# Log-softmax over 50,000 columns: tiles of every second row in place of neighbouring rows, and 40 empty instructions taken out

## The chip, the core and the metric

The kernel runs on one core of one Trainium2 chip. The metric is the device time of the whole program in microseconds (us). The core has five engines with queues of their own (TensorE, VectorE, ScalarE, GpSimd, SyncE) and 16 DMA engines that move data between the chip's memory (HBM) and the on-chip memory (SBUF, 128 partitions).

## The reference

For each of 16 x 512 = 8192 rows of 50,000 float32 numbers, the logarithm of the softmax is computed: the row less its maximum, less the logarithm of the sum of the exponentials.

```python
batch, seq, vocab = 16, 512, 50000

def reference(x):
    max_x = np.max(x, axis=-1, keepdims=True)
    shifted = x - max_x
    log_sum_exp = np.log(np.sum(np.exp(shifted), axis=-1, keepdims=True))
    return (shifted - log_sum_exp).astype(np.float32)
```

The input is 1638.4 MB and the output as much. Each number is read once and written once. The rows are independent, so the order in which they are worked on is free.

## The kernel before

A tile is 32 rows. Each row is cut into G = 4 pieces of 12,500 numbers, so a tile fills 128 partitions with 12,500 numbers (50,000 B) each. There are 256 tiles and four buffers; tile t lives in buffer t modulo 4. SyncE issues the loads, VectorE takes the maxima, ScalarE takes the exponentials with their sums, TensorE adds the sums of the four pieces of a row, VectorE subtracts in place, and ScalarE issues the store.

```python
P = 128
G = 4
R = P // G            # 32 rows in a tile
C = 3125              # a quarter of a partition's 12500 columns
NBUF = 4
NS = 4
GATE = 2
PAUSE = 40
GS = G * NS           # 16 pieces of a row in a part of tile 0
RS = P // GS          # 8 rows in a part of tile 0

def take(engine, sem, n=16, pause=PAUSE):
    engine.wait_ge(sem, n)
    for _ in range(pause):
        engine.nop()
    engine.wait_ge(sem, n).then_inc(sem, -n)
```

`take` is how an engine waits for a transfer: a DMA raises a semaphore by 16 when it is done, and the engine that waits takes the 16 off again.

The views of input and output, whole tiles first and then the parts of tile 0, and the address of tile number 4q + first + i in a loop:

```python
    xt = xf.rearrange("(t r) (g w) -> t (r g) w", r=R, g=G)
    ot = of.rearrange("(t r) (g w) -> t (r g) w", r=R, g=G)
    xs = xf.rearrange("(t s r) (g w) -> t s (r g) w", s=NS, r=RS, g=GS)
    os = of.rearrange("(t s r) (g w) -> t s (r g) w", s=NS, r=RS, g=GS)

    def run(a, first, n):
        part = a[first : first + NBUF * n].rearrange("(q i) p w -> q i p w", i=NBUF)
        return lambda q, i: part[bass.ds(q, 1), i].rearrange("o p w -> (o p) w")
```

The loads. Tile 0 comes in four parts of 8 rows, each with a semaphore of its own, so that work can begin early. A later load into a buffer waits until the buffer's store is done.

```python
        for s in range(NS):
            sync.dma_start(out=bufs[0][:, cols(s)], in_=xs[0, s]).then_inc(landed_part[s], 16)
        for t in range(1, NBUF):
            load(t, xt[t])
        take(sync, stored[0], 16 * NS)
        load(0, xt[NBUF])
        src = run(xt, NBUF + 1, rounds - 1)
        with sync.Fori(0, rounds - 1) as q:
            for i in range(NBUF):
                j = (i + 1) % NBUF
                take(sync, stored[j])
                load(j, src(q, i))
        # ... the last loads and waits
```

VectorE on a tile (ScalarE's exponentials run beside it; TensorE's sums and ScalarE's logarithm come ahead of the subtraction):

```python
        def whole(j, by_pieces=False):
            take(vector, landed[j])
            for c in range(NS):
                vector.tensor_reduce(out=negms[j][:, c : c + 1], in_=bufs[j][:, cols(c)],
                                     op=ALU.max, axis=AX, negate=True)  # ... signals
            # ... the maximum over a row's four pieces, the rescaled sums
            subtract(j, *([bufs[j][:, cols(c)] for c in range(NS)] if by_pieces else [bufs[j]]))
```

ScalarE issues the store of one tile in the middle of its work on the next (`GATE`). Tile 0 is stored in four parts, like its load; the last tile is stored in four column pieces:

```python
        def store(j, dst, buf):
            subtracted.next(scalar.dma_start(out=dst, in_=buf)).then_inc(stored[j], 16)

        def whole(j, dst=None):
            for c in range(NS):
                if c == GATE and dst is not None:
                    store((j - 1) % NBUF, dst, bufs[(j - 1) % NBUF])
                # ... the exponential of a quarter, with its sum
            # ... scale, logarithm

        def in_parts(j, t):
            for s in range(NS):
                # ... the exponential of a part, with its sum
                if s:
                    store(j, os[t, s - 1], bufs[j][:, cols(s - 1)])
                log(NBUF + s)
            store(j, os[t, NS - 1], bufs[j][:, cols(NS - 1)])
        # ...
        for c in range(NS):
            store(NBUF - 1, ot[ntiles - 1][:, cols(c)], bufs[NBUF - 1][:, cols(c)])
```

Of the kernel before, what the change touches and what calls it, by code (L numbers as in the profile page):

```python
# [16 lines left out]
G = 4  # L17
R = P // G
C = 3125
NBUF = 4  # L20

NS = 4

GATE = 2

PAUSE = 40
GS = G * NS
RS = P // GS

# [16 lines left out]
        self.seen = 0  # L46


def take(engine, sem, n=16, pause=PAUSE):

    engine.wait_ge(sem, n)
    for _ in range(pause):
        engine.nop()
    engine.wait_ge(sem, n).then_inc(sem, -n)  # L54


def cols(c):
    return slice(c * C, (c + 1) * C)
# [3 lines left out]
def kernel(  # L62
# [6 lines left out]
    xf = x.flatten_outer_dims()  # L69
    of = out.flatten_outer_dims()  # L70
# [3 lines left out]
    ntiles = N // R  # L74


    rounds = (ntiles - NBUF) // NBUF
    assert ntiles % NBUF == 0 and rounds >= 2
    tail = range(1 + rounds * NBUF, ntiles)

    xt = xf.rearrange("(t r) (g w) -> t (r g) w", r=R, g=G)
    ot = of.rearrange("(t r) (g w) -> t (r g) w", r=R, g=G)
    xs = xf.rearrange("(t s r) (g w) -> t s (r g) w", s=NS, r=RS, g=GS)
    os = of.rearrange("(t s r) (g w) -> t s (r g) w", s=NS, r=RS, g=GS)

    def run(a, first, n):

        part = a[first : first + NBUF * n].rearrange("(q i) p w -> q i p w", i=NBUF)
        return lambda q, i: part[bass.ds(q, 1), i].rearrange("o p w -> (o p) w")

    data = ctx.enter_context(tc.tile_pool(name="data", bufs=1))
    stats = ctx.enter_context(tc.tile_pool(name="stats", bufs=1))
# [10 lines left out]
    bufs = [data.tile([P, W], FP32, name=f"buf{j}") for j in range(NBUF)]  # L103
# [41 lines left out]
    @block.gpsimd  # L145
    def _(gpsimd):
        k = 0
        for g in (GS, G):
            view = ones[g].rearrange("p (r g) -> p r g", g=g)
            r = P // g  # L150
            gpsimd.memset(ones[g], 1.0).then_inc(ready)
            gpsimd.affine_select(  # L152
                out=view, in_=view, pattern=[[-g, r], [0, g]], base=0,
                channel_multiplier=1, compare_op=ALU.is_ge, fill=0.0,
            ).wait_op(ready, k + 1, "sem-ge").then_inc(ready)
            gpsimd.affine_select(  # L156
                out=view, in_=view, pattern=[[g, r], [0, g]], base=g - 1,
                channel_multiplier=-1, compare_op=ALU.is_ge, fill=0.0,
            ).wait_op(ready, k + 2, "sem-ge").then_inc(ready)
            k += 3  # L160

    @block.sync
    def _(sync):
        def load(j, src):
            sync.dma_start(out=bufs[j], in_=src).then_inc(landed[j], 16)

        for s in range(NS):
            sync.dma_start(out=bufs[0][:, cols(s)], in_=xs[0, s]).then_inc(
                landed_part[s], 16
            )  # L170
        for t in range(1, NBUF):
            load(t, xt[t])
        take(sync, stored[0], 16 * NS)
        load(0, xt[NBUF])
        src = run(xt, NBUF + 1, rounds - 1)
        with sync.Fori(0, rounds - 1) as q:
            for i in range(NBUF):
                j = (i + 1) % NBUF
                take(sync, stored[j])
                load(j, src(q, i))  # L180
        for t in tail:
            take(sync, stored[t % NBUF])
            load(t % NBUF, xt[t])
        for j in range(NBUF - 1):
            take(sync, stored[j])
        take(sync, stored[NBUF - 1], 16 * NS)
# [78 lines left out]
    @block.scalar  # L265
    def _(scalar):
        def log(k):
            added.next(
                scalar.activation(out=logs[k], in_=rowsums[k], func=ACT.Ln)  # L269
            ).then_inc(logged.sem)  # L270
# [9 lines that stand above are left out]
                shifted.next(  # L280
                    scalar.activation(  # L281
                        out=dump, in_=bufs[j][:, cols(c)], func=ACT.Exp,
                        bias=negms[j][:, c : c + 1], scale=1.0,
                        accum_out=parts[j][:, c : c + 1],
                    )
                ).then_inc(on_act.sem)
                on_act.next(scalar.nop())  # L287
            agreed.next(
                scalar.activation(  # L289
                    out=scales[j], in_=negms[j], func=ACT.Exp,  # L290
                    bias=negmaxs[j][:, 0:1], scale=-1.0,
                )
            ).then_inc(rescaled.sem)
            log(j)

        def in_parts(j, t):
            for s in range(NS):
                agreed.next(
                    scalar.activation(  # L299
                        out=dump, in_=bufs[j][:, cols(s)], func=ACT.Exp,  # L300
                        bias=negmaxs[NBUF + s][:, 0:1], scale=1.0,
                        accum_out=sub_sum[:, s : s + 1],
                    )
                ).then_inc(summed_part.sem)
# [5 lines that stand above are left out]
        def settle():  # L310
            for count in (on_act, shifted, agreed, added, subtracted):
                count.settle(scalar)

        nc.scalar.preload_act_table_set("natural_log_exp_and_others")  # L314
        in_parts(0, 0)
        settle()
        whole(1)
        settle()
        dst = run(ot, 1, rounds)
        with scalar.Fori(0, rounds) as q:  # L320
            for i in range(NBUF):
                whole((i + 2) % NBUF, dst(q, i))
            settle()
        for t in tail[1:-1]:
            whole(t % NBUF, ot[t - 1])
        store(t % NBUF, ot[t], bufs[t % NBUF])
        whole(NBUF - 1)
        for c in range(NS):
            store(NBUF - 1, ot[ntiles - 1][:, cols(c)], bufs[NBUF - 1][:, cols(c)])

    @block.tensor
    def _(tensor):
# [58 lines left out]
```

## Time and profile before

| what | value |
|---|---|
| time, median of 3 runs | 7589.43 us (7589.03 to 7601.84) |
| span of the profiled run | 7587.3 us |
| VectorE busy | 5443.2 us |
| ScalarE busy | 3184.8 us |
| TensorE busy | 478.3 us |
| HBM read and written | 1638.40 MB each |
| mean rate of the DMA engines | 432 GB/s |
| loads of a whole tile | 255, median 36.7 us from issue to landing |
| loads of a part of tile 0 | 4, median 11.2 us |
| stores of a whole tile | 254, median 41.7 us |
| stores of a part | 8, median 18.8 us |

An engine's busy time is the sum of its instructions' durations; waits are not in it. A line of a group of instructions names the source line (L226), the engine (DVE is VectorE, ACT ScalarE, PE TensorE; SPq, DVEq and ACTq are the queues of SyncE, VectorE and ScalarE), the operation, what it writes and reads, and how often it ran. The share of the DMA queues is the time that their packets took, as a share of the span of all 16 DMA engines. A transfer is made of packets: here one per partition with the partition's data, and small ones that signal that it is done.

### The profile page before, as it was taken

The numbers are of one execution on the slowest core, as the hardware profiler recorded it, in microseconds if no ns is written. First come the engines' busy times: TensorE is split into PE (matmuls) and PEld (weight loads), VectorE is DVE, ScalarE is ACT, GpSimd is POOL, SyncE is SP. The second block draws the span as 40 slices with busy tenths as digits, with TensorE's granted clock in tenths as the row PEclk, the third lists the DMA queues.
The fourth block names the chain that finished last, engine by engine and source line by source line (L and its number), as shares of the span: only waits on it lengthen the run. The fifth ranks groups of instructions, "written<-read, shape, count | busy, mean of one in ns | idle before, by whom it ended". The sixth has DMA issues, their size and how long they took to land. (4 is left out here: it accounts for less than half of the span.)

```text
span 7587.3 us, 13839 instructions
## 1 busy us (share of the span) xinstructions
PE 478.3 (6%) x2048; PEld 456.1 (6%) x2048; DVE 5443.2 (72%) x2832; ACT 3184.8 (42%) x2563; POOL 2.3 (0%) x10
## 2 busy tenths in 40 slices
PE   0000000000000000000000000000000000000000
PEld 0000000000000000000000000000000000000000
DVE  7777777777777777777777777777777777777776
ACT  4344443444434434444443444434444343444433
POOL 0000000000000000000000000000000000000000
DMA  9999999999999999999999999999999999999999
GB/s 423 433 434 434 434 434 433 433 433 434 434 433 432 434 432 434 434 431 434 432 433 432 432 434 431 434 434 430 434 432 433 434 431 434 433 431 434 432 433 398
DMA packets 75026, 3276.85 MB, mean 432 GB/s; under 512 B 8336, under 2 KB 8336, under 8 KB 8336
## 3 DMA queue, kind: packets, MB, share of 16 engines
q10 hardware_dynamic: 37728, 1638.42, 50.0%
q1 hardware_dynamic: 37296, 1638.42, 50.0%
q14 instruction: 2, 0.02, 0.0%
HBM read 1638.40 MB, written 1638.40 MB: 432 GB/s over the span
## 5 line engine op out<-in xcount | busy, mean ns | idle before, releaser
L281 ACT ACTIVATE dump<-buf,negm 128x3125 f32<-128x3125 f32 x1020 | 2925.8, 2868 | 3788.6 <-DVE negm L226 3750.3
L226 DVE TENSOR_REDUCE negm<-buf 128x1 f32<-128x3125 f32 x1020 | 3404.9, 3400 | 913.9 <-DVEq L54 913.9
L214 DVE TENSOR_SCALAR buf<-buf,negmax,logsum 128x12500 f32<-128x12500 f32 (+1 forms) x262 | 1739.5, 6640 | 553.8 <-ACT logsum L269 553.8
L335 PE MATMUL sums<-scaled,ones 128*128 128x1 f32 x2040 | 475.9, 355 | 7056.0 <-DVE scaled L237 7056.0
L335 PEld LDWEIGHTS sums<-scaled,ones 128*128 128x128 f32 x2040 | 454.1, 328 | 7077.9 <-DVE scaled L237 7077.9
L237 DVE TENSOR_TENSOR scaled<-scale,part 128x4 f32<-128x4 f32 x255 | 41.4, 162 | 578.1 <-ACT scale L289 578.1
L269 ACT ACTIVATE logsum<-sums 128x1 f32<-128x1 f32 x259 | 44.3, 171 | 551.7 <-PE sums L335 548.9
L281 ACT ACTIVATION_READ_ACCUMULATOR dump<-buf,negm 128x1 f32 x1020 | 190.1, 186 | 0.0
L289 ACT ACTIVATE scale<-negm,negmax 128x4 f32<-128x4 f32 x255 | 75.8, 297 | 23.5
L231 DVE TENSOR_REDUCE negp<-negm 128x1 f32<-128x4 f32 x255 | 39.9, 157 | 39.0 <-DVE negm L226 39.0
L209 DVE STREAM_TRANSPOSE negmax<-spread 128x32 f32<-128x32 f32 x259 | 54.8, 212 | 9.0
L193 DVE STREAM_TRANSPOSE allneg<-negp 128x32 f32<-128x32 f32 x259 | 54.8, 211 | 9.0
L196 DVE TENSOR_REDUCE rowneg<-allneg 128x8 f32<-128x32 f32 (+1 forms) x259 | 48.1, 186 | 9.0
L203 DVE COPY spread<-rowneg 128x32 f32<-128x32 f32 x259 | 46.8, 181 | 9.0
L244 DVE TENSOR_REDUCE negp<-buf 128x1 f32<-128x3125 f32 x4 | 13.6, 3403 | 7.5 <-DVEq L54 7.5
L299 ACT ACTIVATE dump<-buf,negmax 128x3125 f32<-128x3125 f32 x4 | 11.5, 2870 | 14.4 <-DVE negmax L209 14.4
L346 PE MATMUL sums<-sub_sum,ones 128*128 128x1 f32 x8 | 2.3, 362 | 29.5 <-ACT dump L299 29.5
L346 PEld LDWEIGHTS sums<-sub_sum,ones 128*128 128x128 f32 x8 | 2.0, 312 | 29.8 <-ACT dump L299 29.8
L314 ACT ACT_TABLE_LOAD x1 | 1.3, 1283 | 1.0 <-SPq L123 1.0
L152 POOL TENSOR_SCALAR_AFFINE_SELECT ones<-ones 128x128 f32<-128x128 f32 x2 | 0.9, 442 | 0.1
L156 POOL TENSOR_SCALAR_AFFINE_SELECT ones<-ones 128x128 f32<-128x128 f32 x2 | 0.9, 428 | 0.1
L299 ACT ACTIVATION_READ_ACCUMULATOR dump<-buf,negmax 128x1 f32 x4 | 0.7, 186 | 0.0
(5 smaller groups left out, 0.8 us busy)
## 6 DMA issues: line engine op xcount, KB each, us to landing
buf<-in_x_dram SPq DMA_DIRECT2D x255, 6250.0 KB, 36.7
out_dram<-buf ACTq DMA_DIRECT2D x254, 6250.0 KB, 41.7
out_dram<-buf ACTq DMA_DIRECT2D x8, 1562.5 KB, 18.8
buf<-in_x_dram SPq DMA_DIRECT2D x4, 1562.5 KB, 11.2
```

The costliest lines, as they stand in the source:

```text
L193: vector.transpose(out=allneg, in_=negp.to_broadcast([P, SQ]))
L196: vector.tensor_reduce(out=rowneg[:, : SQ // g], in_=allneg.rearrange("p (r g) -> p r g", g=g), op=op, axis=AX, negate=negate,)
L203: vector.tensor_copy(out=spread.rearrange("p (r g) -> p r g", g=g), in_=rowneg[:, : SQ // g, None].to_broadcast([P, SQ // g, g]),)
L209: vector.transpose(out=negmaxs[k], in_=spread)
L214: ins = vector.tensor_scalar(out=buf, in0=buf, scalar1=negmaxs[k][:, 0:1], scalar2=logs[k], op0=ALU.add, op1=ALU.subtract,)
L226: vector.tensor_reduce(out=negms[j][:, c : c + 1], in_=bufs[j][:, cols(c)], op=ALU.max, axis=AX, negate=True,).then_inc(shifted.sem if c < ...
L231: vector.tensor_reduce(out=negp, in_=negms[j], op=ALU.min, axis=AX).then_inc(on_dve.sem)
L237: vector.tensor_mul(out=scaleds[j], in0=scales[j], in1=parts[j])
L269: scalar.activation(out=logs[k], in_=rowsums[k], func=ACT.Ln)
L281: scalar.activation(out=dump, in_=bufs[j][:, cols(c)], func=ACT.Exp, bias=negms[j][:, c : c + 1], scale=1.0, accum_out=parts[j][:, c : c + 1],
L289: scalar.activation(out=scales[j], in_=negms[j], func=ACT.Exp, bias=negmaxs[j][:, 0:1], scale=-1.0,)
L335: ins = tensor.matmul(rowsums[j], ones[G], scaleds[j][:, c : c + 1], start=c == 0, stop=c == NS - 1,)
```

## The change

The 40 empty instructions in `take` go, with the first of its two waits. And a tile no longer holds 32 neighbouring rows: of each 64 rows, the even-numbered ones make one tile and the odd-numbered ones the next. The same holds for the four parts of tile 0. On chip all is as before: 128 partitions of 12,500 numbers, four partitions to a row, the same engine work and the same number of transfers. What differs is the order of the addresses that a transfer walks through in HBM, and how its pattern is written. The pause was a delay between the end of a transfer and the next use of its buffer; the rows taken alternately are another way of placing what is in flight at one time.

```diff
-PAUSE = 40
...
-def take(engine, sem, n=16, pause=PAUSE):
-
-    engine.wait_ge(sem, n)
-    for _ in range(pause):
-        engine.nop()
+def take(engine, sem, n=16):
+
     engine.wait_ge(sem, n).then_inc(sem, -n)
...
-    xt = xf.rearrange("(t r) (g w) -> t (r g) w", r=R, g=G)
-    ot = of.rearrange("(t r) (g w) -> t (r g) w", r=R, g=G)
-    xs = xf.rearrange("(t s r) (g w) -> t s (r g) w", s=NS, r=RS, g=GS)
-    os = of.rearrange("(t s r) (g w) -> t s (r g) w", s=NS, r=RS, g=GS)
-
-    def run(a, first, n):
-
-        part = a[first : first + NBUF * n].rearrange("(q i) p w -> q i p w", i=NBUF)
-        return lambda q, i: part[bass.ds(q, 1), i].rearrange("o p w -> (o p) w")
+
+    def combs(a):
+        both = a.rearrange("(t r h) (g w) -> h t r g w", h=2, r=R, g=G)
+        return [both[t % 2, t // 2] for t in range(ntiles)], both
+
+    (xt, xh), (ot, oh) = combs(xf), combs(of)
+    xs, os = (
+        a.rearrange("(t s r h) (g w) -> h t s r g w", h=2, s=NS, r=RS, g=GS)[0]
+        for a in (xf, of)
+    )
+
+    def run(both, first, n):
+
+        k = NBUF // 2
+
+        def tile_of(q, i):
+            h, t = (first + i) % 2, (first + i) // 2
+            part = both[h, t : t + k * (n - 1) + 1 : k]
+            return part[bass.ds(q, 1)].rearrange("o r g w -> (o r) g w")
+
+        return tile_of
...
-        src = run(xt, NBUF + 1, rounds - 1)
+        src = run(xh, NBUF + 1, rounds - 1)
...
-        dst = run(ot, 1, rounds)
+        dst = run(oh, 1, rounds)
...
-            store(NBUF - 1, ot[ntiles - 1][:, cols(c)], bufs[NBUF - 1][:, cols(c)])
+            store(NBUF - 1, ot[ntiles - 1][:, :, cols(c)], bufs[NBUF - 1][:, cols(c)])
```

## The prediction

> **What bounds the kernel now.** I read the page from the top: the busy times, the slices, the queues, then the waits, then the table by stage, then the source lines that the change touches.
>
> ```profile
> span 7587.3 us, 13839 instructions
> PE 478.3 (6%) x2048; PEld 456.1 (6%) x2048; DVE 5443.2 (72%) x2832; ACT 3184.8 (42%) x2563; POOL 2.3 (0%) x10
> ...
> DMA  9999999999999999999999999999999999999999
> ...
> DMA packets 75026, 3276.85 MB, mean 432 GB/s; under 512 B 8336, under 2 KB 8336, under 8 KB 8336
> ...
> q10 hardware_dynamic: 37728, 1638.42, 50.0%
> q1 hardware_dynamic: 37296, 1638.42, 50.0%
> ```
>
> No compute engine is above 72%, but the two DMA queues together take 100.0% of the time of 16 DMA engines: loads (q1) and stores (q10) share them half and half. The next view says whether that is so in every stage (columns as labelled: length, busy time per engine, clock, DMA share, GB/s).
>
> ```profile
> 10.00:110.00 100.00, 7.94 (x32) 7.35 (x32) 79.48 (x57) 49.96 (x42) 0.00 (x0) 1.00 1.01 426
> 110.00:1000.00 890.00, 56.00 (x240) 53.43 (x240) 642.86 (x331) 373.03 (x300) 0.00 (x0) 1.00 1.00 434
> 1000.00:7000.00 6000.00, 377.15 (x1617) 359.84 (x1617) 4307.22 (x2232) 2524.10 (x2029) 0.00 (x0) 1.00 1.00 433
> 7000.00:7540.00 540.00, 35.32 (x152) 33.69 (x152) 388.05 (x199) 224.00 (x181) 0.00 (x0) 1.00 1.00 433
> 7540.00:7588.00 48.00, 1.86 (x8) 1.78 (x8) 23.09 (x15) 12.44 (x10) 0.00 (x0) 1.00 0.68 291
> ```
>
> From 10 to 7540 us the DMA engines have no idle time. One tile is 6.4 MB in and 6.4 MB out, and 12.8 MB at 434 GB/s is 29.5 us; the timeline near 3020 us shows VectorE starting a new tile at 3019.51 and the next at 3049.04, 29.53 us apart. So the pace is that of the transfers, and one DMA engine moves 434 / 16 = 27.1 GB/s. Only the last 48 us have free DMA time, about 15 us of it.
>
> ```profile
> DVE negm L226 <- DVEq L54: 913.9, 252, 4.4
> ```
>
> VectorE waits 3.6 us a tile for a landing: it is early, never late.
>
> ```profile
> L54 DVEq EVENT_SEMAPHORE  x259: 49/50/50, 7.4 to 7544.7; - x130
> L54 SPq EVENT_SEMAPHORE  x256: 27/28/28, 78.7 to 7586.0; - x128
> ```
>
> This is the last line of `take`, one record for each call: 259 calls on VectorE, 256 on SyncE. The empty instructions ahead of it would be 40 x 515 = 20,600 records, more than the 13,839 instructions of the whole page. The list of built instructions agrees: the kernel before holds none of these 40 on either engine. The build dropped them, since they carry no wait and no signal. The pause isn't there to be removed.
>
> [...] 259 loads and 262 stores are 521 transfers, and 521 x 16 = 8336 is just the number of packets under 512 B. [...]
>
> **The change, part by part.**
>
> *The pause:* 0 instructions removed from what runs. 0 us.
>
> *The whole tiles (255 loads, 254 stores).* The HBM side goes from 128 pieces of 50,000 B in a row to 32 rows x 4 pieces of 50,000 B, with a row skipped after each. The built instructions show the HBM pattern as 32 x 4 x 12500 against 128 x 12500 in SBUF. [...] the pieces stay 50,000 B, and so do the bytes. By the same 27.1 GB/s this costs 0 us. The pattern has one more dimension; if issuing it takes longer, that lies on the queues of SyncE, which waits 7431 us of the span, and of ScalarE, where an issue takes 0.34 us now and the engine is 42% busy. Even twice that is hidden behind VectorE's 3.6 us of waiting.
>
> *Tile 0, loaded and stored in four parts.* A part is now 8 rows x 16 pieces of 3125 elements (12,500 B), every second row, against 128 partitions. The slowest dimension on the HBM side is 8. Before it was 128, as neighbouring rows merged. [...] The bytes of tile 0 are 12.8 MB in all:
> - before, each of 16 engines carried 12.8 / 16 = 0.8 MB of it;
> - after, each of 8 engines carries 12.8 / 8 = 1.6 MB and the other 8 carry none.
>
> So eight engines have 0.8 MB more to move: 0.8 MB / 27.1 GB/s = 29.5 us, half in loads and half in stores. The other eight have 29.5 us less.
>
> Is it on the path? Every later tile needs all 16 engines before it counts as landed or stored. A lag of eight engines is therefore made good only if these eight have idle time later, and the stage table gives them none up to 7540 us. Nor can the lag starve them: a load takes 36.7 us from issue to landing and a store 41.7 us, while each alone needs 6.4 MB / 434 GB/s = 14.7 us, so about 22 + 27 = 49 us a tile is queueing. The slow eight always have a transfer queued; the fast eight will have gaps. The final tile keeps its split into 16 (its HBM side is 32 x 4 x 3125), and the chain at the end isn't changed.
>
> Sum: 7589.4 + 0 + 0 + 29.5 = 7619 us, 0.4% more.
>
> **The rivals.**
>
> *A. The split stays at 16 in tile 0 too* (software or the issuing sequencer reshapes 8 x 16 into 128). For it: 8 x 16 pieces are 128 pieces, the same as the SBUF side. Against: the built instruction carries 8 as its first size. Then nothing is left of the change: 7589 us, give or take 3.
>
> *B. HBM dislikes the rows.* Tiles 2t and 2t+1 now cover the same 12.8 MB in turns, so a load and the next walk the same region. [...] Against: each piece is still a 50,000 B run[...]. A gain is ruled out by the 100.0%: if every idle DMA microsecond vanished, only some 20 to 25 us of head and tail are there. A loss of 1% would be 7665 us, of 5% 7970 us.
>
> *C. The spread over partitions changes with the extra dimension.* [...] For it: before was a plain 128 x 12500 pattern, and after isn't. Against: 4 pieces make one row, so 32 rows can be dealt out like 32 groups of 4 partitions. [...] in tile 0 alone it would make the 8-engine parts slower still, perhaps twice, so 7650 us.
>
> *D. The lag is partly recovered,* because the last 48 us have about 15 us of free DMA time. Against: that gap comes from the last tile's compute, which starts when the late engines land it, so it moves with the lag. At best some microseconds: 7605 to 7615 us.
>
> **Range and chances.** My main line at 7619 us takes about 55%, A about 20%, D and a worse tile 0 about 15%, a loss through B or C in every tile about 10%. So the range of 8 in 10 runs from just under A, 7586, to 7655 us. Faster by over 2% (under 7437 us) [...]. I give 0.01. Slower by over 2% needs B or C in every tile: 0.09. Within 2%: 0.90.
>
> **What would show it.** (a) Packets under 512 B: 8 transfers x 8 fewer completions, so 8336 - 64 = 8272 if k = 8, and 8336 under A. (b) The four part loads: median issue to landing 11.2 us now; on 8 engines each part takes 1.6 MB / 217 GB/s = 7.4 us instead of 3.7, so the second and third landing come 2 and 3 times 3.7 us later, and the median should go to 11.2 + 9.2 = 20 us. (c) The mean DMA share from 1000 to 7000 us about 0.996 instead of 1.00, and 431 to 432 GB/s. (d) The whole loads and stores keep some 37 and 42 us. (e) VectorE and ScalarE rows keep their mean times. I am wrong if the DMA rate in the steady stage falls by more than 1% (B or C), or if 8336 stays (A), or if the 64 completions are gone and the time still doesn't move, which would mean that the eight engines did have room.

## The result, and the profile after

| | before | after |
|---|---|---|
| time, median of 4 runs each | 7590.06 us | 7663.06 us |
| ratio | | 1.0096 (95% interval 1.0078 to 1.0113) |

The change makes the kernel 73 us slower. I had put it at 7619 us, with 7655 us as the upper end.

The page of the kernel after, from the top:

```profile
span 7659.5 us, 13839 instructions
PE 478.5 (6%) x2048; PEld 456.3 (6%) x2048; DVE 5443.6 (71%) x2832; ACT 3184.9 (42%) x2563; POOL 2.3 (0%) x10
...
DMA  8999999999999999999999999999999999999999
GB/s 254 432 433 434 434 432 433 434 432 433 433 433 433 432 434 433 432 434 434 431 434 431 433 434 432 434 432 433 434 433 433 434 432 434 434 433 433 434 433 403
DMA packets 74962, 3276.85 MB, mean 428 GB/s; under 512 B 8272, under 2 KB 8272, under 8 KB 8272
...
q1 hardware_dynamic: 37264, 1638.42, 50.1%
q10 hardware_dynamic: 37696, 1638.42, 49.6%
```

Engines, instructions and bytes are as before; 64 small packets are gone. Of 40 slices only the first stands out: 254 GB/s. The same stretches as in the prediction (length, busy time of each engine, clock, DMA share, GB/s), with one more row for the longer end:

```profile
10.00:110.00 100.00, 2.35 (x8) 2.01 (x8) 28.69 (x26) 13.84 (x13) 0.00 (x0) 1.00 0.94 223
110.00:1000.00 890.00, 56.02 (x240) 53.45 (x240) 636.68 (x331) 372.36 (x301) 0.00 (x0) 1.00 0.98 422
1000.00:7000.00 6000.00, 379.05 (x1624) 361.67 (x1624) 4313.54 (x2234) 2523.84 (x2030) 0.00 (x0) 1.00 1.00 433
7000.00:7540.00 540.00, 33.61 (x144) 32.06 (x144) 390.56 (x201) 230.76 (x185) 0.00 (x0) 1.00 1.00 433
7540.00:7588.00 48.00, 3.73 (x16) 3.56 (x16) 31.28 (x20) 17.95 (x16) 0.00 (x0) 1.00 1.00 433
7588.00:7660.00 72.00, 3.73 (x16) 3.56 (x16) 42.84 (x25) 24.87 (x20) 0.00 (x0) 1.00 0.81 349
```

The row of 1000 to 7000 us is what it was, share and rate. From 10 to 110 us the DMA engines count as busy for 94% of the time and yet move 223 GB/s, where before moved 426: busy and slow. The start in four stretches shows where the loss lies, first for before, then for after:

```profile
0.00:50.00 50.00, 2.35 (x8) 2.01 (x8) 36.15 (x28) 22.17 (x18) 2.29 (x10) 1.00 0.97 404
50.00:100.00 50.00, 3.73 (x16) 3.56 (x16) 40.56 (x23) 22.88 (x21) 0.00 (x0) 1.00 1.01 423
100.00:145.00 45.00, 3.73 (x16) 3.56 (x16) 32.97 (x20) 18.63 (x16) 0.00 (x0) 1.00 1.00 434
145.00:250.00 105.00, 5.78 (x25) 5.52 (x26) 77.08 (x43) 49.57 (x39) 0.00 (x0) 1.00 1.00 431
```

```profile
0.00:50.00 50.00, 0.59 (x2) 0.50 (x2) 10.18 (x11) 6.37 (x5) 2.30 (x10) 1.00 0.93 151
50.00:100.00 50.00, 1.76 (x6) 1.50 (x6) 13.88 (x13) 7.56 (x9) 0.00 (x0) 1.00 0.98 275
100.00:145.00 45.00, 1.87 (x8) 1.78 (x8) 34.71 (x17) 21.45 (x17) 0.00 (x0) 1.00 0.54 226
145.00:250.00 105.00, 7.47 (x32) 7.12 (x32) 67.85 (x39) 40.73 (x34) 0.00 (x0) 1.00 0.98 402
```

Two losses can be told apart, measured against the 434 GB/s of the steady stage. *Idle* is length x (1 - share). *Slow packets* is length x (share - rate / 434). For after, the first 50 us give 50 x (1 - 0.93) = 3.5 us idle and 50 x (0.93 - 151 / 434) = 29.1 us slow. The third stretch is the opposite: share 0.54, so half of the engines stand still, and the others run at full rate (226 of 234 GB/s). The four stretches together:

| | idle, us | slow packets, us |
|---|---|---|
| before | 1.0 | 4.4 |
| after | 27.3 | 52.9 |
| difference | 26.3 | 48.5 |

The sum of the differences, 74.8 us, is the 73 us of the result, to within the two digits of the share. The idle part is what I had predicted; the slow packets are what I had not. They show in the part loads too. This is the timeline's first maximum of each part of tile 0 (start, duration, instruction, and in brackets the wait before it):

```profile
22.89 3.41 DVE L251 TENSOR_REDUCE negp<-buf 128x1 f32<-128x3125 f32 x1 [22.89 <-DVEq L49]
43.70 3.41 DVE L251 TENSOR_REDUCE negp<-buf 128x1 f32<-128x3125 f32 x1 [16.48 <-DVEq L49]
63.54 3.41 DVE L251 TENSOR_REDUCE negp<-buf 128x1 f32<-128x3125 f32 x1 [13.71 <-DVEq L49]
86.46 3.41 DVE L251 TENSOR_REDUCE negp<-buf 128x1 f32<-128x3125 f32 x1 [16.79 <-DVEq L49]
```

A part of 1.6 MB comes in every 20 to 23 us, where eight engines at 27.1 GB/s would need 7.4 us. In the trace's packet records a part packet of 12,500 B takes 0.47 us in before. Here, beside the load of tile 1, it takes 0.9 to 1.5 us, most often 1.4; the 50,000 B packets of tile 1 take about 5.0 us in place of 1.85.

### The profile page after: what moved, and what is told of

It is laid out like the page before. It is cut to its first block, busy times and chain, and to the rows that moved or that the text cites. A ratio compares the mean times of both kernels' runs of the same rounds, so it can differ in the third digit from the quotient of the medians.

```text
span 7659.5 us, 13839 instructions
## 1 busy us (share of the span) xinstructions
PE 478.5 (6%) x2048; PEld 456.3 (6%) x2048; DVE 5443.6 (71%) x2832; ACT 3184.9 (42%) x2563; POOL 2.3 (0%) x10
## 2 busy tenths in 40 slices
DMA packets 74962, 3276.85 MB, mean 428 GB/s; under 512 B 8272, under 2 KB 8272, under 8 KB 8272
```

## The experiments

Two theories for the slow packets. **SBUF:** each of the eight engines writes 16 neighbouring partitions one after another, and engines meet on the same way into SBUF. **HBM:** rows two apart, read in step, collide in HBM. Each run below stands beside the kernel before on the same chip. The times of before itself run from 7566 to 7695 us here; the intervals are wide for that reason, and a ratio is not the quotient of the two medians beside it. Two of the traces below (every second row but not in tile 0, and tile 0 like any other) are of executions that took 7725 and 7661 us and lost the time after the first 250 us, so the start of the traces is used beside the times.

### The pause alone

```diff
-PAUSE = 40
+PAUSE = 0
```

> The kernel before with PAUSE = 0, rows untouched: the other part of the change alone. If the build dropped the 40 empty instructions, as the record count of before says: 7590 us within 0.2%, VectorE waiting about 3.6 us a tile as before. Rival: the pause does run and something of the 73 us comes from taking it away: then 7600 us or more.

Measured: 7587.79 us against 7584.96; ratio 1.0031 (0.9992 to 1.0069). The built instructions are those of before, except for labels, and the page again has 13839 instructions. This part of the change does nothing.

### Every second row, but not in tile 0

```diff
-        both = a.rearrange("(t r h) (g w) -> h t r g w", h=2, r=R, g=G)
-        return [both[t % 2, t // 2] for t in range(ntiles)], both
+        plain = a.rearrange("(t r) (g w) -> t (r g) w", r=R, g=G)
+        both = a[R : N - R].rearrange("(t r h) (g w) -> h t r g w", h=2, r=R, g=G)
+        inner = [both[t % 2, t // 2] for t in range(ntiles - 2)]
+        return [plain[0]] + inner + [plain[ntiles - 1]], both
...
-        a.rearrange("(t s r h) (g w) -> h t s r g w", h=2, s=NS, r=RS, g=GS)[0]
+        a.rearrange("(t s r) (g w) -> t s (r g) w", s=NS, r=RS, g=GS)
...
-            h, t = (first + i) % 2, (first + i) // 2
+            h, t = (first - 1 + i) % 2, (first - 1 + i) // 2
...
```

> The kernel after, but tile 0 (and the last tile) hold neighbouring rows again, so that the four parts of tile 0 go out as 128 pieces in a row; tiles 1 to 254 still take every second row. If the whole 73 us come from the parts of tile 0 (whatever the reason inside them): 7590 us within 0.2%. If reading every second row in step is slow by itself at the start, in the whole tiles 1 to 3 too: 7605 to 7640 us, with whole-tile packets well over 1.85 us in the first 80 us.

Measured: 7570.78 us against 7584.96; ratio 1.0001 (0.9958 to 1.0043). With 254 of 256 tiles still of every second row, the loss is gone: the interval leaves room for some 33 us, not for 73. In the four stretches of the start its trace has 404, 427, 431 and 433 GB/s, as before has. The loss sits in tile 0.

### Neighbouring rows everywhere, but parts of every fourth row

```diff
-    xs = xf.rearrange("(t s r) (g w) -> t s (r g) w", s=NS, r=RS, g=GS)
-    os = of.rearrange("(t s r) (g w) -> t s (r g) w", s=NS, r=RS, g=GS)
+    xs = xf.rearrange("(t r s) (g w) -> t s r g w", s=NS, r=RS, g=GS)
+    os = of.rearrange("(t r s) (g w) -> t s r g w", s=NS, r=RS, g=GS)
```

> The kernel before, but part s of tile 0 takes rows s, s+4, ... of the first 32 rows; all whole tiles hold neighbouring rows. The parts are again 8 rows x 16 pieces, so 8 engines and 16 partitions each, but the rows lie 800,000 B apart instead of 400,000. Theory SBUF (8 engines with 16 neighbouring partitions each collide on the way into SBUF): as slow as after, 7650 to 7670 us, part packets again 1.3 to 1.4 us. Theory HBM (rows 400,000 B apart, read in step, collide in HBM): another number, 7615 to 7645 us, and other packet times. Only the imbalance of the eight engines, nothing slower: 7619 us.

Measured: 7662.56 us; ratio 1.0109 (1.0068 to 1.0150). This is the kernel before with nothing changed but the rows of four loads and four stores, and it has the whole loss, with the 40 empty instructions still in the source. The stretch from 8 to 50 us:

```profile
8.00:50.00 42.00, 0.59 (x2) 0.50 (x2) 9.59 (x11) 4.32 (x4) 0.00 (x0) 1.00 1.00 153
```

The kernel after has 154 GB/s in that stretch. Doubling the distance of the rows changes nothing, which speaks against the HBM theory.

### Tile 0 like any other

```diff
-        for s in range(NS):
-            sync.dma_start(out=bufs[0][:, cols(s)], in_=xs[0, s]).then_inc(
-                landed_part[s], 16
-            )
+        load(0, xt[0])
...
-        take(sync, stored[0], 16 * NS)
+        take(sync, stored[0])
...
-        in_parts(0, 0)
+        whole(0)
...
-        whole(1)
+        whole(1, ot[0])
```

(and the same on VectorE and TensorE)

> The kernel after, but tile 0 is loaded, worked on and stored like any other tile, every second row, without the four parts: all transfers on 16 engines. If 8 engines (with whatever follows from it) cause the loss: 7590 to 7605 us; some 5 to 15 us over before since the first work starts later. If it is the distance of the rows in HBM: still over 7620 us, with slow packets in the first 80 us.

Measured: 7590.57 us; ratio 1.0042 (1.0006 to 1.0077). All 16 engines start in step on rows two apart, and the rate from 4 to 60 us is full:

```profile
4.00:60.00 56.00, 1.87 (x8) 1.78 (x8) 35.46 (x20) 22.46 (x17) 0.00 (x0) 1.00 1.01 428
```

The HBM theory falls for whole tiles: reading every second row on 16 engines isn't slow (428 GB/s here; before has 431 from 4 to 60 us). What is slow is a load on eight engines, and the next two runs ask whether eight engines are enough for that.

### Part loads into 32 or 64 partitions in place of 128

```diff
-            sync.dma_start(out=bufs[0][:, cols(s)], in_=xs[0, s]).then_inc(
-                landed_part[s], 16
-            )
+            for j in range(NS):
+                sync.dma_start(
+                    out=bufs[0][32 * j : 32 * j + 32, cols(s)],
+                    in_=xs[0, s][:, 4 * j : 4 * j + 4, :],
+                ).then_inc(landed_part[s], 16)
...
-                take(vector, landed_part[s])
+                take(vector, landed_part[s], 16 * NS)
```

(with 64: two transfers of 8 pieces into 64 partitions each; if a pattern is dealt out in its order, as the SBUF theory takes it, an engine then writes 4 or 8 neighbouring partitions at a time)

> The kernel after, but each part of tile 0 is loaded by four transfers of 8 rows x 4 pieces into 32 partitions each[...]. Same bytes from the same HBM rows on the same 8 engines. The pieces lie in other partitions than the sums assume, so the 32 rows of tile 0 are not normalized rightly; all work is still done. Theory SBUF (the eight meet in SBUF because each walks 16 neighbouring partitions): part packets drop from 1.4 us to about 0.5 to 0.7 us, the loads of tile 1 beside them run near 1.85 us, and only the imbalance stays: some 30 us over before. Theory of 8 engines alone (any transfer on 8 of 16 engines is slow when read at row distance): part packets stay at 1.3 to 1.4 us and the time at over 60 us more than before.

> The same with two transfers of 8 rows x 8 pieces into 64 partitions[...]. What is left out is the same as in the run with 32. Theory SBUF: between the two, part packets 0.6 to 1.0 us, 35 to 60 us over before. Theory of 8 engines alone: 1.3 to 1.4 us, over 60 us more.

Measured: with 32, 7632.42 us against 7589.48, ratio 1.0041 (1.0015 to 1.0066); with 64, 7658.82 us, ratio 1.0071 (1.0045 to 1.0098). With 32, the same bytes come from the same rows in the same order, again by eight engines (packets under 512 B: 8368, the 8272 of after and 8 for each of 12 more transfers), and some 30 us of the loss are gone: 43 us are left by the medians, 31 by the ratio. Four short stretches of its trace:

```profile
4.00:13.00 9.00, 0.00 (x0) 0.00 (x0) 1.34 (x1) 0.00 (x0) 0.00 (x0) 1.00 0.50 214
...
15.00:22.00 7.00, 0.58 (x2) 0.50 (x2) 0.85 (x5) 3.16 (x3) 0.00 (x0) 1.00 1.00 223
22.00:25.50 3.50, 0.00 (x0) 0.00 (x0) 2.65 (x1) 0.00 (x0) 0.00 (x0) 1.00 1.09 443
...
70.00:100.00 30.00, 1.87 (x8) 1.78 (x8) 25.28 (x13) 13.27 (x11) 0.00 (x0) 1.00 0.50 217
```

First row: eight engines alone, half the share, and half the full rate (214 of 434 GB/s); they are no longer in each other's way. Second and third row: tile 1 comes in beside them. By the order of the part transfers and their packets' times (the records don't name partitions), partitions 64 to 127 are written until about 22 us and partitions 0 to 63 after it. In the first case all 16 engines together reach half the rate, in the second the full one (in so short a stretch the share is rough). So the loads of tile 1 are disturbed when a part goes to the upper half (packets of 3.4 to 3.9 us, where I had expected them near 1.85 throughout), and not when it goes to the lower. Same rows, eight engines each time, transfers of the same size: the place in SBUF decides. Last row: the lag is worked off by eight engines at full rate while eight stand idle.

With 64 I expected 35 to 60 us and got 69 by the medians (54 by the ratio): transfers into 64 partitions are nearly as bad as those into 128. In the packet records its part packets take 0.96 or 1.4 us in turns, as one half of the partitions follows the other.

### The parts alone

```diff
+        take(sync, stored[0], 16 * NS)
         for t in range(1, NBUF):
             load(t, xt[t])
-        take(sync, stored[0], 16 * NS)
```

> The kernel after, but the loads of tiles 1 to 3 are issued only when the four parts of tile 0 are stored, so that the parts have the DMA engines to themselves; the total is of no interest (some 60 to 110 us longer). If the eight engines are in each other's way by themselves (SBUF): part packets about 0.93 us, 15 us between the landings of two parts. If they are slow only beside the loads of the other engines: 0.47 us and 7.5 us.

Measured: 7656.34 us in one run, 67 us over before. The stretch with nothing but part loads:

```profile
5.00:35.00 30.00, 0.59 (x2) 0.50 (x2) 6.50 (x6) 3.16 (x3) 0.00 (x0) 1.00 0.51 116
```

Eight engines are busy and move 116 GB/s, 14.5 each, so a part packet takes 12,500 / 14.5 = 0.86 us; the run with 32 has 214 GB/s in the same situation. The eight do hinder each other, about two to one. Even so, having the rest wait costs no more than letting all compete: the total of this one run is about that of after.

### Loads or stores alone on eight engines

```diff
-    xs, os = (
-        a.rearrange("(t s r) (g w) -> t s (r g) w", s=NS, r=RS, g=GS)
-        for a in (xf, of)
-    )
+    xs = xf.rearrange("(t s r h) (g w) -> h t s r g w", h=2, s=NS, r=RS, g=GS)[0]
+    os = of.rearrange("(t s r) (g w) -> t s (r g) w", s=NS, r=RS, g=GS)
```

(against the run with neighbouring rows in tile 0; for the stores, the other way round on the kernel after)

> The kernel with tile 0 of neighbouring rows (edges_plain), but the four part loads read every second row of the first 64, so they alone go out on 8 engines; the four part stores stay on 16. Tile 0's output rows then hold the results of other input rows; all work is done. Theory: half of the imbalance, 14.7 us, and nearly all of the collisions on the way into SBUF, some 40 us: 50 to 65 us over before. If the loss belongs to loads and stores alike: about 37 us.

> The kernel after, but the four part loads read 32 neighbouring rows on 16 engines; the four part stores alone go out on 8. Tile 0's output rows hold the results of other input rows. Theory: half of the imbalance, 14.7 us, and little more, since stores read SBUF where the part loads write it and are spread in time: 12 to 25 us over before. If loads and stores share the loss alike: about 37 us.

> The kernel after once more, beside the two halves on the same chip: 73 us over before as measured first, and about the sum of the two halves if they add up.

Measured against 7589.42 us: loads 7648.83 (+59 us), ratio 1.0065 (1.0027 to 1.0102); stores 7611.83 (+22 us), ratio 1.0026 (1.0002 to 1.0051); after 7668.96 (+80 us), ratio 1.0069 (1.0031 to 1.0108). By the medians the halves add up: 59 + 22 = 81. By the ratios they give 0.65% + 0.26% = 0.91% against 0.69%, which the intervals allow, so the sum holds only roughly. The four stretches of the loads' run:

```profile
0.00:50.00 50.00, 0.65 (x3) 0.56 (x3) 10.19 (x11) 7.44 (x6) 2.29 (x10) 1.00 0.96 161
50.00:100.00 50.00, 1.70 (x6) 1.44 (x6) 13.89 (x13) 6.50 (x7) 0.00 (x0) 1.00 0.97 299
100.00:145.00 45.00, 3.09 (x14) 3.01 (x14) 35.62 (x21) 24.70 (x19) 0.00 (x0) 1.00 0.76 312
145.00:250.00 105.00, 8.12 (x36) 7.69 (x35) 84.65 (x44) 49.81 (x41) 0.00 (x0) 1.00 0.99 424
```

and of the stores':

```profile
0.00:50.00 50.00, 2.35 (x8) 2.01 (x8) 37.15 (x28) 22.91 (x19) 2.29 (x10) 1.00 0.97 404
50.00:100.00 50.00, 3.73 (x16) 3.56 (x16) 40.31 (x22) 22.64 (x19) 0.00 (x0) 1.00 0.81 307
100.00:145.00 45.00, 1.87 (x8) 1.78 (x8) 9.90 (x8) 5.69 (x6) 0.00 (x0) 1.00 0.91 356
145.00:250.00 105.00, 5.60 (x24) 5.34 (x24) 73.67 (x36) 43.29 (x34) 0.00 (x0) 1.00 0.98 408
```

and of the run with 32 partitions:

```profile
0.00:50.00 50.00, 1.75 (x6) 1.50 (x6) 16.18 (x17) 10.77 (x10) 2.29 (x10) 1.00 0.84 265
50.00:100.00 50.00, 2.45 (x10) 2.28 (x10) 33.34 (x20) 16.43 (x14) 0.00 (x0) 1.00 0.71 307
100.00:145.00 45.00, 3.73 (x16) 3.56 (x16) 35.07 (x21) 24.04 (x20) 0.00 (x0) 1.00 0.84 296
145.00:250.00 105.00, 5.60 (x24) 5.34 (x24) 64.94 (x34) 37.30 (x30) 0.00 (x0) 1.00 0.99 423
```

By the two formulas above, less what before loses in the same stretches:

| over before, us | idle | slow packets | sum |
|---|---|---|---|
| part loads on 8 | 14.4 | 42.3 | 56.7 |
| part stores on 8 | 16.2 | 10.9 | 27.1 |
| both (after) | 26.3 | 48.5 | 74.8 |
| both, loads by 32 partitions | 29.8 | 15.9 | 45.7 |

The idle term is 14 to 16 us for each half, and most of the slow packets belong to the loads.

## Why the prediction missed

**The pause: right.** 0 us predicted; without it the built program is the same apart from labels, and the rows of tile 0 alone have the whole loss.

**The whole tiles: right.** 0 us predicted; with only tile 0 (and the last tile) put back, the ratio is 1.0001, and the kernel after moves 433 GB/s from 1000 to 7000 us, as before does.

**Eight engines in tile 0: right.** 8272 packets under 512 B were predicted for k = 8, k being the number of engines that share a part transfer; 8272 are on the page: 513 transfers of a tile or of a piece of the last tile with 16 each, and 8 of a part of tile 0 with 8 each. With nothing but part loads under way the DMA share is 0.51 (the run with the parts alone). Rival A is out.

**The lag and its size: right.** Predicted 29.5 us, half of it for loads and half for stores; measured as idle time 14.4 and 16.2 us, and 29.8 us where the collisions are mostly taken away. It isn't made good later, as predicted against rival D. What I had wrong is where it shows: not a share of 0.996 over the whole run but eight engines standing still between 100 and 145 us. After that the lag is worked off, and from 1000 us on the share is 1.00.

**The step that failed** is the rate of the eight. "0.8 MB / 27.1 GB/s = 29.5 us" and, in sign (b), "1.6 MB / 217 GB/s = 7.4 us" take each of them at the full rate of a 16-engine transfer, and the loads beside them as undisturbed. In the run with the parts alone they moved 14.5 GB/s each. Beside tile 1 all 16 engines together moved 151 GB/s in the first 50 us, and a part came in every 20 to 23 us. So the sum lacked 48 us of slow packets, and 7619 should have read about 7665. None of the three signs of being wrong that the prediction ends with came true: they look at the steady stage, at the 64 packets and for a time that stands still, not at the rate of the parts themselves.

The cause, as far as the runs go: the slow packets depend on where the eight engines write in SBUF. With nothing beside them, the part loads move 116 GB/s as they stand, 129 with transfers into 64 partitions (from 4 to 7 us), and 214 with transfers into 32, near the 217 of eight engines at full rate. In the run with 32 and tile 1 beside them, all 16 engines together move 223 GB/s or 443, by the half of the partitions that a part goes to. I infer from the order of the pattern that each engine gets 16 neighbouring partitions, or 8 with 64 and 4 with 32, and that the longer walks make the engines meet on the way into SBUF; the trace names neither engines nor partitions, and where they would meet isn't shown. What the parts lose among themselves is only part of the 48 us: by the packets of the parts alone, 64 packets x (0.86 - 0.47) us are 25 us on half of the engines, so about 12 us (an estimate). The stores' run shows another 10.9 us; what is left comes with the loads of tile 1 beside the part loads.

**Rival C was nearest.** That the spread over partitions matters is what the runs point to, but I tied it to the extra dimension of the pattern; the whole tiles have the same dimension and run at full rate (433 GB/s from 1000 to 7000 us). Its aside on tile 0 ("slower still, perhaps twice, so 7650 us") is what happened, but nearly three times beside other loads, not twice. **Rival B is out** by the full-rate run of tile 0 as a whole (428 GB/s), and by the run with 32 partitions, in which eight engines read the same rows in the same order (214 GB/s).

What stays open: how the parts and the load of tile 1 slow each other down. In the kernel after, the packets of tile 1 take about 5.0 us where 1.85 is the full rate, and those of the parts beside them 0.9 to 1.5 us where they take 0.86 with nothing beside them. Why both lose isn't shown, and no run here separates them. About 11 to 16 us of slow packets also remain in the stores' run and in the run with 32; their cause isn't shown.

## What to carry to other kernels

When a rearranged view no longer merges neighbouring rows, look at the first size that the built DMA instruction carries: here it fell from 128 to 8, eight DMA engines got nothing, and in a kernel bound by transfers the others' extra bytes went straight into the time (26 of the 75 us). Then ask how the remaining engines are spread over the partitions: here a load on half of the engines ran at about a quarter of the rate (116 of 434 GB/s; 214 with the same rows in transfers into 32 partitions), and slowed down what ran beside it (packets of 5.0 us in place of 1.85). A busy DMA share with a low rate (0.93 and 151 GB/s) is the sign of the second, a share near one half with full rate per engine (0.54 and 226 GB/s) that of the first.

## What the hardware showed that I had not expected

A load on eight engines into 128 partitions got 116 GB/s alone, while eight engines at full rate move 217. And a DMA took longer to issue with a pattern of three dimensions. The source line of the whole-tile loads in the kernel after (shortest, median and longest time on SyncE's queue, in ns):

```profile
L172 SPq DMA_DIRECT2D buf<-in_x_dram x255: 534/538/7576, 4.0 to 7580.3; - x128
```

The run with parts of every fourth row, where the whole tiles still have two dimensions, shows 333 ns at the median. On ScalarE's queue it is 554 ns against 338. Here it is hidden: with these patterns in 254 tiles, the run with neighbouring rows in tile 0 has no loss.
